# One PSUM bank or two for the two blocks of products of a weight tile, and four transposes ahead of their evictions

## The chip, the cores and the metric

The kernel runs on one core of a Trainium2 chip. The metric is the device time of one execution in microseconds (us); where several executions were timed, their median is given.

## The reference

Two blocks of two layers each, over one sequence of 256 tokens of width 1024. The first mixes a gated convolution with neighbourhood attention and ends each layer with a feed-forward part (dense in layer 0, eight experts with the best two taken in layer 1). The second has a window-and-context attention and a two-way matrix LSTM, and carries a context stream of another 256 tokens beside the latent one. Cut to what the change touches:

```
def first_block(x, p, ...):                       # layer i
    proj = h @ w_in[i] + b_in[i]                  # a, g (convolution), q, k, v
    conv_out = conformer_conv(a, g, ...)          # u = a * sigmoid(g), 31 taps
    attn_out = neighbourhood_attention(q, k, v, rpb[i])
    ...
def moe_swiglu(x, w_router, w1, w3, w2):          # layer 1: 8 experts
    y = (silu(xb @ w1[e]) * (xb @ w3[e])) @ w2[e]
    ...
def hybrid_layer(x, ctx, ..., last):
    xn = rmsnorm(x, norm_g) * (1 + scale_x) + shift_x
    cn = rmsnorm(ctx, norm_g) * (1 + scale_c) + shift_c
    aq, ak, av, az, mq, mk, mv, mo, mz, mi, mf = project(xn, w_in)
    caq, cak, cav, caz, cmq, cmk, ... = project(cn, w_in)
    q = rope_2d(aq); k = rope_2d(ak)
    att_x = window_ctx_attention(q, k, v, kc, vc, sink) * silu(az)
    xq, xk = silu(dwconv([mq, mk], conv_w, conv_b))     # 5 taps
    h_lat = mlstm_bidir(xq, xk, mv, mi, mf, ctx_state)
    ...
```

## The kernel before, in words

Every float32 product is made of three products of rounded parts: high by high, high by low and low by high (`mm3`). Weights come as raw tiles of 1 MB by DMAs that SyncE (SP) issues (L326). ScalarE (ACT) writes the high part, `whi` (L340), and VectorE (DVE) the low part, `wlo` (L341), in pieces of 1024 columns; two or three such split tiles exist at a time.

Where the result is wanted with channels on the partitions, a split tile of 1024 x 256 goes through `wstat`. It holds two blocks of 128 output channels, and each block is 8 x 3 = 24 products `gT` of 128x256, accumulated in PSUM. Then an eviction reads the block: ACT's sigmoid or DVE's `u` (L700) in the two mixers of the first block, ACT's `qraw` (L1633) for the queries and ACT's `up` (L1682) for the LSTM's q and k in the second. 45 weight tiles go this way, so there are 90 blocks: 16 tiles in the two mixers, 11 for the context (nine in its layer 0, two in its layer 1), 18 in the two latent layers of the second block.

The banks of `gT` come from the ring "a" of four PSUM banks (`bank`). Before the change, one bank is taken per weight tile and its halves hold the two blocks. Other products use the same ring: the token-major projections `gk`, the output projection `go`, the gates.

The order on each engine is fixed when the program is built: a scheduler places the instructions by priorities (`lift` raises those of evictions and of the chains behind them), and each engine runs its list in order. Where two engines touch one PSUM bank, the later one waits for the earlier on a semaphore. Behind the query blocks a rotation product (`prope`, of `qraw`) goes to GpSimd (POOL; `rt`, L1593) and to ACT (`Q`, L1601). Behind the LSTM blocks DVE runs the five taps. In the mixers DVE runs 31 taps (`y`, L765) as work that fills its gaps, and the taps left over go through `cvu`, a copy of `u` made by 16 DMAs (L783), to products `pcy`.

The context's layers run inside the expert layer of the first block: experts' weights (`sraw`, four buffers of 1 MB) stream in all the while, and their products `su` and `sy` fill TensorE's gaps. The context's norm, `norm_T`, is called once per context layer. It turns the normalized rows with transposes `ptT`, four to a bank over four banks, and ACT (`xhi`, L1502) and DVE (`xu`, L1503) read each half of a bank (256 columns, two transposes).

Of the kernel before, what the change touches and what calls it, by code (L numbers as in the profile page):

```python
# [23 lines left out]
P = 128  # L24
T = 256
# [145 lines left out]
class Kern:  # L171
# [201 lines left out]
            yield 1, lambda p0=p0: self.wload(w2d, 0, 8, c0 + p0, 256), lambda w, p0=p0: self.wstat(w, X, evict, p0 // P)  # L373

    def wstat(self, w, X, evict, b0):
        pt = self.bank("a", "gT")
        for bb in range(2):
            ps, cs = pt[:, bb * 256:(bb + 1) * 256], slice(bb * P, (bb + 1) * P)
            for k in range(8):
                self.mm3(ps, w[0][:, k, cs], w[1][:, k, cs], X.hi[:, k], X.lo[:, k], k == 0, k == 7)  # L380
            while self.pend:
                self.pend.popleft()[1]()
            with self.lift():
                evict(b0 + bb, ps)
# [1098 lines left out]
    def norm_T(self, l, s, x, xn, X, tag, keep=None):  # L1483


        nc, mods = self.nc, self.mods[l]
        if s:
            for t in range(2):
                self.rms(x[:, t], xn[t], self.hp.tile([P, D], F32, name="junk", tag="pT"))
        for j in range(4):  # L1490
            pt = self.bank(tag, "ptT")
            ks = slice(2 * j, 2 * j + 2)
            if keep is None:
                u = self.hp.tile([P, 512], F32, name="xu", tag="AT", bufs=2).rearrange("p (k t) -> p k t", k=2)
            else:
                u = keep[:, ks]
            for kk in range(2):
                k = 2 * j + kk
                a, b, ps = mods[:, s, 8 + k:9 + k], mods[:, s, k:k + 1], pt[:, kk * T:(kk + 1) * T]
                for t in range(2):  # L1500
                    self.turn_(ps[:, t * P:(t + 1) * P], xn[t][:, k * P:(k + 1) * P], self.ident)
                nc.scalar.activation(X.hi[:, k], ps, AF.Identity, scale=a, bias=b)  # L1502
                nc.vector.tensor_scalar(u[:, kk], ps, a, b, op0=ALU.mult, op1=ALU.add)  # L1503
            nc.vector.tensor_sub(X.lo[:, ks], u, X.hi[:, ks])
# [724 lines left out]
```

## Time and profile before

| | us |
|---|---|
| three runs | 2059.68, 2062.71, 2063.76 |
| their median | 2062.71 |
| the profiled execution, its own time | 2059.87 |
| its span, first to last instruction | 2058.1 |

The profiled execution is one more execution beside the three; all durations quoted from the trace are its own. Its span leaves 1.8 us outside. TensorE (PE) is busy for 93% of the span, DVE for 67%, ACT for 49%, POOL for 4%. The mean granted clock of TensorE is 0.972 of full speed.

### The profile page before, as it was taken

What the parts mean: (1) busy time and instruction counts of PE and PEld (TensorE: products, weight loads), DVE (VectorE), ACT (ScalarE), POOL (GpSimd) and SP (SyncE); (2) the same over time, 40 slices, a digit from 0 to 9 for tenths busy, and PEclk for the clock granted to TensorE, in tenths of its full rate; (3) what the DMA queues carried; (4) which work ended last, traced back from release to release, by engine and by line L of the source; (5) the groups of instructions that cost most, each with busy time, mean ns of one, the idle gap of its engine ahead of it and who ended that gap; (6) DMA issues with size and microseconds to landing.
All of it is one profiled execution on the core that took longest, in us unless ns stands there. A gap on an engine that the chain in (4) does not pass through costs nothing. (4 is left out here: it accounts for less than half of the span.)

```text
span 2058.1 us, 34210 instructions
## 1 busy us (share of the span) xinstructions
PE 1913.0 (93%) x13442; PEld 1526.5 (74%) x13442; DVE 1374.8 (67%) x2557; ACT 1012.2 (49%) x1663; POOL 81.8 (4%) x164
## 2 busy tenths in 40 slices
PE   6999999899887899788999999999999988998997
PEld 6768889687655565556877887887887868876886
DVE  8767444786646535564444444888888888887977
ACT  4534444335424323243333334777767745865774
POOL 1000000100100000000000000000000012011100
PEclk9999999899899999999999999999999999999999
DMA  8558776653689899999999996999999964334330
GB/s 291 171 187 295 265 263 207 204 188 123 231 343 324 305 357 305 342 370 350 370 381 394 377 340 244 342 353 328 353 332 336 326 202 141 103 109 123 103 103 32
DMA packets 276315, 541.06 MB, mean 263 GB/s; under 512 B 10912, under 2 KB 124336, under 8 KB 275888
## 3 DMA queue, kind: packets, MB, share of 16 engines
q1 hardware_dynamic: 274736, 534.73, 74.3%
q0 software_dynamic: 1120, 3.72, 0.6%
q8 instruction: 108, 1.77, 0.4%
q14 instruction: 63, 0.52, 0.1%
q10 hardware_dynamic: 288, 0.33, 0.0%
HBM read 533.26 MB, written 1.05 MB: 260 GB/s over the span
## 5 line engine op out<-in xcount | busy, mean ns | idle before, releaser
L341 DVE TENSOR_TENSOR wlo<-wraw,whi 128x1024 fp32r<-128x1024 f32 x572 | 681.9, 1230 | 184.7 <-ACT whi L340 181.2
L340 ACT ACTIVATE whi<-wraw 128x1024 fp32r<-128x1024 f32 x572 | 574.9, 1052 | 258.1 <-PE gT L353 47.5
L353 PE MATMUL gT<-xhi,whi 128*128 128x256 f32 x720 | 216.1, 302 | 19.7 <-ACT up L1682 8.6
L353 PE MATMUL gT<-xhi,wlo 128*128 128x256 f32 x720 | 209.9, 293 | 2.8 <-DVE wlo L341 2.7
L353 PE MATMUL gT<-xlo,whi 128*128 128x256 f32 x720 | 210.3, 293 | 1.7 <-DVE xlo L452 0.9
L353 PEld LDWEIGHTS gT<-xhi,whi 128*128 128x128 f32 x720 | 141.8, 197 | 33.6 <-ACT up L1682 10.2
L353 PEld LDWEIGHTS gT<-xhi,wlo 128*128 128x128 f32 x720 | 141.5, 197 | 8.7 <-issue 4.9
L353 PEld LDWEIGHTS gT<-xlo,whi 128*128 128x128 f32 x720 | 142.1, 197 | 5.4 <-issue 2.5
L353 PE MATMUL su<-sraw,xs 128*32 128x256 f32 (+1 forms) x2048 | 126.6, 371 | 15.2 <-DMA sraw<-in_moe_w 14.6
L353 PE MATMUL h<-whi,xeh 128*128 128x512 f32 x336 | 131.6, 392 | 1.0 <-DVE z L1183 1.0
L353 PE MATMUL h<-wlo,xeh 128*128 128x512 f32 x336 | 131.7, 392 | 0.0
L353 PE MATMUL h<-whi,xel 128*128 128x512 f32 x336 | 131.5, 391 | 0.0
L353 PE MATMUL hps<-xeh,whi 128*128 128x256 f32 x448 | 128.1, 286 | 0.0
L353 PE MATMUL hps<-xel,whi 128*128 128x256 f32 x448 | 126.7, 283 | 0.0
L353 PE MATMUL hps<-xeh,wlo 128*128 128x256 f32 x448 | 126.6, 283 | 0.0
L353 PEld LDWEIGHTS su<-sraw,xs 128*32 128x32 f32 x2048 | 59.1, 113 | 61.7 <-DMA sraw<-in_moe_w 19.2
L919 DVE TENSOR_TENSOR gg<-gg,hps 128x256 f32<-128x256 f32 x50 | 20.9, 419 | 122.1 <-ACT gg L918 122.1
L353 PE MATMUL gk<-whi,xhi 128*128 128x512 f32 x240 | 99.7, 418 | 2.1 <-ACT whi L340 1.5
L353 PE MATMUL gk<-wlo,xhi 128*128 128x512 f32 x240 | 98.7, 411 | 2.4 <-DVE wlo L341 2.2
L353 PE MATMUL hps<-xhi,whi 128*128 128x256 f32 x352 | 100.2, 285 | 0.0
L353 PE MATMUL hps<-xlo,whi 128*128 128x256 f32 x352 | 99.6, 283 | 0.0
L353 PE MATMUL hps<-xhi,wlo 128*128 128x256 f32 x352 | 99.5, 283 | 0.0
(470 smaller groups left out, 3968.6 us busy)
## 6 DMA issues: line engine op xcount, KB each, us to landing
sraw<-in_moe_w SPq DMA_DIRECT2D x168, 1024.0 KB, 8.8
wraw<-in_moe_w SPq DMA_DIRECT2D x168, 1024.0 KB, 6.8
wraw<-in_w_in SPq DMA_DIRECT2D x58, 1024.0 KB, 7.0
wraw<-in_ffn_w SPq DMA_DIRECT2D x33, 1024.0 KB, 5.2
wraw<-in_w_ada SPq DMA_DIRECT2D x24, 1024.0 KB, 5.3
wraw<-in_w_out SPq DMA_DIRECT2D x14, 1024.0 KB, 5.2
wraw<-in_w_in SPq DMA_DIRECT2D x24, 512.0 KB, 5.3
wraw<-in_ple_gate_w SPq DMA_DIRECT2D x8, 1024.0 KB, 7.1
```

The source lines that it names most:

```text
L340: nc.scalar.activation(hi[:, a:b], raw[:, a:b], AF.Copy)
L341: i = nc.vector.tensor_sub(lo[:, a:b], raw[:, a:b], hi[:, a:b])
L353: return self.behind(self.nc.tensor.matmul(out, lhsT, rhs, start=start, stop=stop, **kw))
L919: nc.vector.tensor_mul(g, g, pt[:, 256:])
```

## The change

It changes two helpers. In `wstat`, the line that takes a bank moves into the loop over the two blocks: each block has the first 256 columns of a bank of its own, and the ring of four turns twice as fast. In `norm_T`, all four transposes of a bank are written ahead of its two pairs of evictions, where two transposes and their evictions stood before the next two.

```
     def wstat(self, w, X, evict, b0):
-        pt = self.bank("a", "gT")
         for bb in range(2):
-            ps, cs = pt[:, bb * 256:(bb + 1) * 256], slice(bb * P, (bb + 1) * P)
+            ps, cs = self.bank("a", "gT")[:, :T], slice(bb * P, (bb + 1) * P)
             for k in range(8):
                 self.mm3(ps, w[0][:, k, cs], w[1][:, k, cs], X.hi[:, k], X.lo[:, k], k == 0, k == 7)
             while self.pend:
...
             for kk in range(2):
+                k, ps = 2 * j + kk, pt[:, kk * T:(kk + 1) * T]
+                for t in range(2):
+                    self.turn_(ps[:, t * P:(t + 1) * P], xn[t][:, k * P:(k + 1) * P], self.ident)
+            for kk in range(2):
                 k = 2 * j + kk
                 a, b, ps = mods[:, s, 8 + k:9 + k], mods[:, s, k:k + 1], pt[:, kk * T:(kk + 1) * T]
-                for t in range(2):
-                    self.turn_(ps[:, t * P:(t + 1) * P], xn[t][:, k * P:(k + 1) * P], self.ident)
                 nc.scalar.activation(X.hi[:, k], ps, AF.Identity, scale=a, bias=b)
                 nc.vector.tensor_scalar(u[:, kk], ps, a, b, op0=ALU.mult, op1=ALU.add)
```

Each engine has the same instructions in the same number before and after (14503 on PE, 2175 on ACT, 3217 on DVE, 173 on POOL and 1475 on SP, all kinds counted). Only their order and their waits differ. Lines from 377 to 1493 of the kernel have numbers lower by one after the change, lines past the middle of `norm_T` higher by one.

First place: PE in the second block's latent layer 0, at the first two blocks of the LSTM's q and k (one weight tile), with the rotation `prope` of the last query block between them. The names in brackets are the engines whose semaphores an instruction waits for. Before:

```order
L353 MATMUL gT<-xhi,whi 128x256
L353 MATMUL gT<-xlo,whi 128x256
L353 MATMUL gT<-xhi,wlo 128x256
L353 MATMUL prope<-qraw,const_20867 128x256 [waits DVE_49,Activation_49]
L356 MATMUL pcols<-const_88,rows 128x36 [waits DVE_49]
L356 MATMUL pcols<-const_88,rows 128x36 x2
L353 MATMUL gT<-xhi,whi 128x256 [waits Activation_49]
L353 MATMUL gT<-xlo,whi 128x256
```

The same place after the change:

```order
L353 MATMUL gT<-xhi,whi 128x256
L353 MATMUL gT<-xlo,whi 128x256
L353 MATMUL gT<-xhi,wlo 128x256
L353 MATMUL prope<-qraw,const_20894 128x256 [waits DVE_49,Activation_49]
L353 MATMUL gT<-xhi,whi 128x256
L353 MATMUL gT<-xlo,whi 128x256
L353 MATMUL gT<-xhi,wlo 128x256
L353 MATMUL gT<-xhi,whi 128x256
```

The second block, behind `prope`, no longer waits for ACT, and it stands ahead of the transposes `pcols` (the LSTM's gate rows), which now follow its 24 products.

Second place: ACT in the same stretch of the same layer; `rows` and `r_dl` belong to the gates. Before:

```order
L1633 ACTIVATE qraw<-gT 128x256
L340 ACTIVATE whi<-wraw 128x1024
L1633 ACTIVATE qraw<-gT 128x256
L1601 ACTIVATE Q<-rt 64x256 x2
L1956 ACT_TABLE_LOAD
L1956 ACTIVATE rows<-rows 36x256
L1957 ACTIVATE rows<-rows 36x256
L1959 ACTIVATE r_dl<-r_dl 36x2
L340 ACTIVATE whi<-wraw 128x1024 x2
L1633 ACTIVATE qraw<-gT 128x256
L1601 ACTIVATE Q<-rt 64x256 x4
L1682 ACTIVATE up<-gT 128x256
```

After:

```order
L1634 ACTIVATE qraw<-gT 128x256
L340 ACTIVATE whi<-wraw 128x1024
L1602 ACTIVATE Q<-rt 64x256 x2
L1634 ACTIVATE qraw<-gT 128x256
L1957 ACT_TABLE_LOAD
L1957 ACTIVATE rows<-rows 36x256
L1958 ACTIVATE rows<-rows 36x256
L1960 ACTIVATE r_dl<-r_dl 36x2
L340 ACTIVATE whi<-wraw 128x1024
L1634 ACTIVATE qraw<-gT 128x256
L1602 ACTIVATE Q<-rt 64x256 x4
L1959 ACTIVATE rows<-rows 36x256
```

The eviction `qraw` of the third query block has moved behind the pair `Q`, and a conversion `whi` and the eviction `up` have moved behind the last of the `rows`.

Third place: SP in the mixer of layer 0, where the copies `cvu` of the taps' input are issued; `in_w_in` is the mixer's weight. Before:

```order
L691 DMA z_66<-in_p 128x2x256
L326 DMA wraw<-in_w_in 128x4x512
L783 DMA cvu<-u 32x2x284 x16
L490 DMA row<-in_b_in 128x512
L326 DMA wraw<-in_w_in 128x4x512
```

After:

```order
L690 DMA z_66<-in_p 128x2x256
L782 DMA cvu<-u 32x2x284 x16
L326 DMA wraw<-in_w_in 128x4x512
L489 DMA row<-in_b_in 128x512
L326 DMA wraw<-in_w_in 128x4x512
```

The 16 copies have moved ahead of one weight tile in SP's queue.

## Rows read from the trace of the kernel before

**Rows 1.** Page, part 1: busy time, share of the span, and instructions per engine.
```profile
PE 1913.0 (93%) x13442; PEld 1526.5 (74%) x13442; DVE 1374.8 (67%) x2557; ACT 1012.2 (49%) x1663; POOL 81.8 (4%) x164
```

**Rows 2.** Waits of PE: who, for whom: us in total, times, longest.
```profile
PE su L353 <- DMA sraw<-in_moe_w: 14.6, 13, 1.9
PE gT L353 <- ACT up L1682: 8.6, 6, 3.7
PE gT L353 <- ACT qraw L1633: 4.8, 3, 2.5
PE gT L353 <- DVE u L700: 2.8, 2, 1.6
PE gT L353 <- DVE xlo L1504: 0.8, 1, 0.8
PE gT L353 <- ACT xhi L1502: 0.4, 1, 0.4
```

**Rows 3.** Windows, gT alone: us, PE, PEld, DVE, ACT busy, clock, DMA share, GB/s.
```profile
1728.90:1732.10 3.20, 3.09 (x23) 2.88 (x23) 0.00 (x0) 0.00 (x0) 1.00 1.02 286
1738.70:1743.75 5.05, 4.96 (x24) 4.76 (x24) 0.00 (x0) 0.01 (x1) 0.58 0.43 120
1913.40:1918.10 4.70, 4.63 (x24) 4.42 (x24) 0.00 (x0) 0.01 (x1) 0.64 0.33 94
923.90:928.50 4.60, 4.54 (x24) 4.34 (x24) 0.00 (x0) 0.00 (x0) 0.65 0.52 209
```

**Rows 4.** Windows, all work: the same columns, with POOL's busy time ahead of the clock.
```profile
33.00:63.00 30.00, 27.70 (x224) 26.89 (x224) 29.70 (x52) 13.05 (x18) 2.79 (x1) 1.00 0.57 173
400.00:520.00 120.00, 114.89 (x883) 95.40 (x882) 93.24 (x181) 53.51 (x103) 5.92 (x12) 0.98 0.53 170
585.00:760.00 175.00, 152.74 (x1420) 104.62 (x1420) 87.20 (x227) 60.55 (x141) 4.09 (x24) 0.94 0.91 324
920.00:940.00 20.00, 13.29 (x136) 8.66 (x135) 9.27 (x28) 5.16 (x13) 0.72 (x6) 0.85 0.79 311
1740.00:1780.00 40.00, 39.93 (x298) 35.24 (x299) 37.43 (x92) 31.41 (x69) 1.77 (x14) 0.96 0.33 106
1920.00:1960.00 40.00, 39.45 (x298) 34.11 (x297) 38.23 (x91) 33.02 (x72) 3.31 (x16) 1.00 0.31 103
```

**Rows 5.** Timeline, mixer of layer 0: start, us, engine, instruction [idle before, releaser].
```profile
51.08 10.38 SPq L783 DMA_DIRECT2D cvu<-u  x16
...
67.02 0.62 PE L353 MATMUL pcy<-cvu,cvw 128*32 128x256 f32 x2
...
81.95 0.39 PE L353 MATMUL gk<-whi,xhi 128*128 128x512 f32 x1
```

**Rows 6.** Page, part 6, DMA issues: count, KB each, median us to landing.
```profile
wraw<-in_w_in SPq DMA_DIRECT2D x58, 1024.0 KB, 7.0
...
cvu<-u SPq DMA_DIRECT2D x32, 71.0 KB, 2.1
```

**Rows 7.** Timeline, context layer 1, its last block of `gT`.
```profile
923.53 0.36 ACT L1682 ACTIVATE up<-gT 128x256 f32<-128x256 f32 x1
923.94 0.58 PE L353 MATMUL gT<-xhi,whi 128*128 128x256 f32 x1 [3.14 <-ACT up L1682]
...
933.25 0.66 PE L356 MATMUL pk<-const,kc 128*128 128x128 f32 x4 [0.36 <-DVE gcols L1967]
```

**Rows 8.** Timeline, latent layers 0 (first four rows) and 1 (last row).
```profile
1728.72 0.86 ACT L1601 ACTIVATE Q<-rt 64x256 fp32r<-64x256 f32 x2 [3.06 <-POOL rt L1593]
...
1737.45 0.85 ACT L1601 ACTIVATE Q<-rt 64x256 fp32r<-64x256 f32 x2 [1.15 <-POOL up L1681]
...
1738.33 0.38 ACT L1682 ACTIVATE up<-gT 128x256 f32<-128x256 f32 x1
...
1738.76 0.58 PE L353 MATMUL gT<-xhi,whi 128*128 128x256 f32 x1 [3.73 <-ACT up L1682]
...
1913.46 0.48 PE L353 MATMUL gT<-xhi,whi 128*128 128x256 f32 x1 [2.52 <-ACT qraw L1633]
```

More of the change, by code (lines that the diff above doesn't have):

```diff
@@ L375, in wstat @@
     def wstat(self, w, X, evict, b0):
-        pt = self.bank("a", "gT")
         for bb in range(2):
-            ps, cs = pt[:, bb * 256:(bb + 1) * 256], slice(bb * P, (bb + 1) * P)
+            ps, cs = self.bank("a", "gT")[:, :T], slice(bb * P, (bb + 1) * P)
             for k in range(8):
@@ L1497, in norm_T @@
             for kk in range(2):
+                k, ps = 2 * j + kk, pt[:, kk * T:(kk + 1) * T]
+                for t in range(2):
+                    self.turn_(ps[:, t * P:(t + 1) * P], xn[t][:, k * P:(k + 1) * P], self.ident)
+            for kk in range(2):
                 k = 2 * j + kk
                 a, b, ps = mods[:, s, 8 + k:9 + k], mods[:, s, k:k + 1], pt[:, kk * T:(kk + 1) * T]
-                for t in range(2):
-                    self.turn_(ps[:, t * P:(t + 1) * P], xn[t][:, k * P:(k + 1) * P], self.ident)
                 nc.scalar.activation(X.hi[:, k], ps, AF.Identity, scale=a, bias=b)
```

## The prediction

> **What bounds the kernel now.** I read the page's busy times first, then PE's waits, then windows of the stretches in which `gT` runs, then the timeline around the longest waits. PE is busy for 93% of the span [rows 1], so the kernel is TensorE-bound on the average and a shorter time has to come out of PE's idle 7% or out of products that run slowly. But the stages differ. In the mixer's window 33 to 63 DVE is busy for 29.70 of 30 us; in the context's windows the DMAs are at 0.91, and PE waits 14.6 us in all for `sraw`; in the latent layers DVE has 37.43 and 38.23 of 40 us while PE has nearly as much [rows 2, 4]. So a wait taken from PE is worth its length only where DVE or the DMAs do not set the pace anyway.
>
> PE's waits name what the one bank costs: products of `gT` wait 8.6 us for `up`, 4.8 for `qraw` and 2.8 for `u`, 16.2 us in 11 waits [rows 2]. The releasers are the evictions of the block before, and the timeline shows the shape: `up` ends at 1738.71, and the first product starts at 1738.76 after 3.73 us of idling [rows 8].
>
> Behind the long waits the products also run slowly. 24 products take 4.96, 4.63 and 4.54 us at a granted clock of 0.58 to 0.65, where 23 took 3.09 at 1.00 [rows 3]. For 24 that is 3.09 x 24 / 23 = 3.22, so the three long waits cost 1.74 + 1.41 + 1.32 = 4.5 us more. At clock 0.58 most of the block ran at the lower of the two levels (1.2 of 2.4 GHz), and what PE did before the fall was to idle 3.73 us.
>
> **The change part by part.** No instruction is added or removed, so nothing has a cost of its own; only waits and order count.
>
> *Own banks.* Before, a tile's second block waits for the eviction of the block just before it. After, a block waits for the one four blocks back. The latest eviction that I rest on is the `up` of 1738.33; it was held up by `Q` at 1737.45, which waits for POOL [rows 8]. Four banks give an eviction three blocks, 3 x 3.22 = 9.7 us, before anyone waits for it, so I take the new bank waits as 0. The faster ring could reach `gk` and `go`, which take two or four banks, but their last bank waited for the last block's eviction before as well: 0.
>
> *norm_T.* The transposes no longer wait for the evictions of the same bank. Products beside the two norms wait 0.8 us for `xlo` and 0.4 for `xhi` [rows 2]; I count 1.2 us in context layer 0 and nothing in layer 1.
>
> *What is on offer, and what I keep, by place.*
>
> Mixer of layer 0: 2.8 us offered (`u`). DVE is full for 30 us there [rows 4], and the products also need DVE's splits. There is a new wait as well: PE's order brings `pcy` some 20 products forward, 20 x 3.22 / 24 = 2.7 us, so with the waits gone it is due at 67.02 - 2.7 - 2.8 = 61.5, while the last copy `cvu` is issued at 61.46 and lands 2.1 us later [rows 5, 6]. That is a wait of up to 2.1, so 0.7 to 2.8 is left; I take 1.5. The weight tile now behind the copies in SP's queue is issued at about 61.5 and lands by 61.5 + 7.0 = 68.5; `gk` starts at 81.95 [rows 5, 6], so it has 13 us and costs nothing. If that cover were gone, the price would be its landing time, 7 us.
>
> Mixer of layer 1: no wait of this kind, 0 offered.
>
> Context layer 0: about 1.8 us of `up`'s 8.6 is left over for the other four waits (8.6 less 3.73 and 3.14, [rows 2, 7, 8]); I place half here, with the norm's 1.2: 2.1 offered. The DMAs are at 0.91 [rows 4]: bounds 0.2 (the other 9%) and 2.1; I take 1.5, because DMAs just below full leave a short wait recoverable.
>
> Context layer 1: 3.14 + 0.5 + 1.32 = 5.0 offered. The DMA share falls to 0.79 in 920 to 940, just where PE idles [rows 4], so about 0.21 x 20 = 4.2 us of DMA time is lost there and could be won. But the tail goes on to `pk` at 933.25, which waits for DVE [rows 7]. Bounds 0 and 5.0; I take half, 2.5.
>
> Latent layer 0: 3.73 + 0.2 + 1.74 = 5.7 offered. The second block now runs ahead of `pcols`, so what is late next is that gate chain, by up to one block (3.2 us), and the third query's `qraw`, which has moved behind a `Q` that waited 3.06 us for POOL [rows 8]. PE has 24 products to run meanwhile, so I put that new wait at 0 to 1.3 us. DVE idles only 2.6 us in 1740 to 1780 [rows 4], which is what can be drawn forward there. Bounds 0 and 5.7; I take 3, DVE's idle time and a little from the stretch ahead.
>
> Latent layer 1: 4.6 + 0.3 + 1.41 = 6.3 offered (of `qraw`, all but 0.2 is here; the last row shows 2.52). DVE idles 1.8 us in 1920 to 1960 [rows 4]. Bounds 0 and 6.3; I take 3, by the same reading.
>
> Sum kept: 1.5 + 1.5 + 2.5 + 3 + 3 = 11.5 us. Sum offered: 2.8 + 2.1 + 5.0 + 5.7 + 6.3 = 21.9 us. The profiled execution would go from 2059.9 to 2048.4. The median of the three runs lies 2.8 us higher, so against it the forecast is 2062.7 - 11.5 = 2051.2, say **2051 us**. The runs span 4.1 us, 0.2%, and that is about what a measurement of this kernel can tell from no change.
>
> **The rivals.**
>
> *All of it is kept.* PE is the bound everywhere and the other engines follow: 2062.7 - 21.9 = 2040.8. For it: PE's 93%. Against it: DVE's 29.70 of 30 and 38.23 of 40, and the full DMA queues [rows 4].
>
> *The wait moves.* DVE, POOL's rotation, `cvu` or the `sraw` stream takes over at each place, and PE idles as long one step later. In the context the order now has 48 `gT` in a row at three places where `su` products stood between the blocks. Those release the `sraw` buffers, so each place may stop the stream for one block: 3 x 3.2 = 9.6 us. With the context's gain gone too (4.0) that is 2062.7 - 7.5 + 9.6 = 2064.8; without it the wait moves for 2062.7. Against it: PE waits for `sraw` [rows 2], so the four buffers are mostly in flight rather than full. Time 2059 to 2066.
>
> *The change does not do what it says*, some other dependence holding the second block. The order shows the wait on ACT gone at the first place in the listing, so I give it nothing beyond the case before.
>
> *Slower, by order.* The scheduler pulls freed blocks ahead of the products on which the slow chains hang: `pcols` in latent layer 0 is an example. Each such block delays a chain by 3.2 us, and if PE then idles for the chain's end, the place loses instead of winning. At the six places where PE now waits longest, 6 x 3.2 = 19.2 against 11.5: 2062.7 + 7.7 = 2070. It decides from five places on (5 x 3.2 = 16 is more than 11.5 + 4.1). For it: ACT's and DVE's full queues in the latent layers. Against it: the queue at PE is not idle meanwhile, and each chain has a block of cover.
>
> *Slower, by the clock.* The blocks go round four banks instead of staying two to a bank, and TensorE's clock falls between them. A block at the low clock costs 1.74 us more [rows 3]. If that came to one block in four, 22 x 1.74 = 38: 2062.7 - 11.5 + 38 = 2089; from nine blocks (9 x 1.74 = 15.7) the change is slower. Against it: in every row with a low clock PE had idled for an eviction first, and in the mixer of layer 1, with no such wait, the clock is 0.98 for 120 us [rows 4].
> The Trainium skill, "TensorE: Matmul & The Clock Gate", section "A second HAM failure mode: psum-queue depth-cycling", is why this rival stands here: it tells of a kernel that cycled through PSUM banks and whose clock swung between its levels because PE idled briefly between groups. By that rule the time would go up; the trace so far agrees with its idling, which the old form has and the new one should lose, and no row shows cycling alone to do it.
>
> **How the numbers follow.** Forecast, part kept: 0.48, with a range of its own of 2046 to 2057 (16 to 6 us of the 21.9). All kept: 0.14. The wait moves: 0.22. Slower by order: 0.10; by the clock: 0.06. Faster by over 0.2% (below 2058.6) is the first two, 0.62; within 0.2%, 0.22; slower, 0.16. The first three cases hold 0.84, and they reach from 2038 (all kept, with the 2.8 us by which executions differ) to 2066, which is the range.
>
> **What would show it.** Right: PE's waits of `gT` for `up`, `qraw` and `u` fall from 16.2 us to under 3; the blocks behind 1738, 1913 and 923 take about 3.2 us at clock 1.00; the latent layers end some 3 us earlier each, and the DMA share at 920 to 940 rises. Wrong on the mixer: `pcy` waits for `cvu` by more than 2 us. Wrong on the latents: `prope`, `pcols` or `sc` wait for ACT, DVE or POOL as long as `gT` did. Wrong on the context: the expert stage is as long as before, with PE waiting longer for `sraw`. The prediction as a whole is wrong if the freed time comes back as DVE or DMA waits in every stage, or if blocks of `gT` run at the low clock with no wait ahead of them.

## The result and the profile after

The changed kernel takes 2051.7 us (median of 6 runs, 2046.4 to 2053.8), the kernel before 2062.2 (6 runs, 2059.7 to 2063.8). The ratio is 0.9943, 95% interval 0.9929 to 0.9956: 11.8 us faster (9.1 to 14.6), where 11.5 was forecast; the two medians lie 10.5 us apart. The profiled execution took 2053.8 us, the slowest of the six, with a span of 2052.0.

The page's first part, which answers to [rows 1]:

```profile
PE 1912.5 (93%) x13442; PEld 1532.2 (75%) x13442; DVE 1373.8 (67%) x2557; ACT 1012.0 (49%) x1663; POOL 81.7 (4%) x164
```

PE's waits after the change (product, releaser: us in total, times, longest). The groups of [rows 2] for `up`, `qraw`, `u` and the context's `xlo` and `xhi` are gone; these are what `gT` still waits for, and the chief waits of other products that are new or longer:

```profile
PE su L353 <- DMA sraw<-in_moe_w: 15.6, 12, 2.5
...
PE prope L353 <- ACT qraw L1634: 4.4, 3, 2.4
PE gT L353 <- DVEq L1090: 4.1, 1, 4.1
...
PE pdec L353 <- DVE dg L1971: 3.6, 1, 3.6
...
PE gT L353 <- DVE wlo L341: 3.3, 3, 1.3
...
PE pk L356 <- DVE gcols L1968: 2.6, 1, 2.6
...
PE sc L353 <- DVE gcols L1968: 1.6, 1, 1.6
PE gT L353 <- ACT whi L340: 1.5, 2, 1.3
...
PE sc L353 <- DVE rt L1592: 1.4, 1, 1.4
...
PE pcols L356 <- ACT rows L1959: 1.2, 1, 1.2
```

So some 17 us of waits went, and some 12 came up elsewhere: `prope`, `pdec`, `pk`, `sc` (for `gcols` and `rt`) and `pcols` have 14.8 us, and had 2.6 before. The windows say where that matters (us, then PE, PEld, DVE, ACT, POOL busy, granted clock, DMA share, GB/s). The first two answer to rows of [rows 4]; as the changed kernel is some 7 us ahead at the start of the context's layer 1 and 10 at its end, the third shows about the work that stood at 920 to 940 before:

```profile
33.00:63.00 30.00, 29.70 (x240) 27.54 (x239) 29.96 (x55) 11.49 (x17) 2.88 (x1) 1.00 0.55 165
920.00:940.00 20.00, 13.54 (x127) 6.22 (x120) 6.00 (x16) 2.40 (x6) 0.46 (x2) 0.77 1.01 373
910.50:930.50 20.00, 15.52 (x172) 10.08 (x171) 11.66 (x35) 6.11 (x15) 0.72 (x6) 0.91 0.99 376
1700.00:1745.00 45.00, 37.68 (x273) 34.66 (x273) 39.20 (x95) 27.59 (x55) 12.83 (x21) 0.92 0.37 109
```

In the mixer PE went from 27.70 to 29.70 of 30 us, with DVE as full as before. For the work of 920 to 940 before, the DMA share rose from 0.79 to 0.99 and PE's busy time from 13.29 to 15.52 us. In the stretch 1700 to 1745 of latent layer 0 PE still idles 7.3 us of 45.

Since each run below left a trace too, a stage's length can be read in 14 executions, as the time between the first starts of two products in the timeline (the first transposes and the first `hps` bound mixer 0; the last `hps` of layer 0 and the first `plg` mixer 1; the 48th of the 96 `go` of the context's layer 0 and the 1201st `hps` the context's layer 1 with its tail; the first latent `pgate` and the transposes at 1870 latent layer 0; the rest is latent layer 1). Worked out from the timelines, means in us:

```
stage               one bank per tile   a bank per block   difference
mixer 0             165.6 (5 traces)    160.0 (8)          -5.6
mixer 1             156.3 (5)           155.2 (8)          -1.1
context layer 1     116.9 (4)           113.1 (8)          -3.8
latent layer 0      179.9 (8)           180.8 (3)          +0.9
latent layer 1      188.2 (8)           190.5 (3)          +2.3
```

(The context's rows have the new norm beside the new banks. Kernels of the last experiments are in a row only where they leave its stage as the whole change or as before.) Within a row and column the traces of the latent layers agree to 1 us, those of the mixers to 3.4, those of the context to 4. The context's layer 0, from the first `su` to the same `go`, isn't listed: with the change it took 293 to 297 us in four traces and 305 to 306 in four, against 299 to 300 before, and one kernel showed both. It goes with TensorE's clock, whose mean over the stage is 0.931 to 0.942 in the four short ones and 0.894 to 0.900 in the four long ones. Among the traces at 0.931 or 0.932 the old form took 298.9, 299.0 and 299.3 us and the new one 296.7, 295.9 and 296.1: 2.9 us less.

### The profile page after: what moved, and what is told of

Its sections match the earlier page's. It is cut to its first block, busy times and chain, and to the rows that moved or that the text cites. A ratio compares the mean times of both kernels' runs of the same rounds, so it can differ in the third digit from the quotient of the medians.

```text
span 2052.0 us, 34198 instructions
## 1 busy us (share of the span) xinstructions
PE 1912.5 (93%) x13442; PEld 1532.2 (75%) x13442; DVE 1373.8 (67%) x2557; ACT 1012.0 (49%) x1663; POOL 81.7 (4%) x164
## 5 line engine op out<-in xcount | busy, mean ns | idle before, releaser
L353 PE MATMUL gT<-xhi,whi 128*128 128x256 f32 x720 | 211.6, 296 | 1.5 <-ACT whi L340 1.5
L353 PE MATMUL su<-sraw,xs 128*32 128x256 f32 (+1 forms) x2048 | 126.4, 374 | 16.1 <-DMA sraw<-in_moe_w 15.6
```

Source lines behind the costliest of these rows:

```text
L353: return self.behind(self.nc.tensor.matmul(out, lhsT, rhs, start=start, stop=stop, **kw))
```

## The experiments

All ratios are to the kernel before, on the same chip and in the same session.

**Parts by place.** `wstat` gets a word for its caller, and only the named callers take a bank per block. The order on PE is that of before with no caller named, and that of the change with all:

```
-    def wstat(self, w, X, evict, b0):
+    def wstat(self, w, X, evict, b0, part):
+        own = part in ("mix",)            # e2: ("ctx",)  e3: ("lat",)  e4, e6: ("ctx", "mix")
         for bb in range(2):
-            ps, cs = self.bank("a", "gT")[:, :T], slice(bb * P, (bb + 1) * P)
+            if own or bb == 0:
+                pt = self.bank("a", "gT")
+            lo = 0 if own else bb * 256
+            ps, cs = pt[:, lo:lo + 256], slice(bb * P, (bb + 1) * P)
```

The first, the mixers alone (A is the theory that the time comes where the traces part, B the forecast's own terms, C scatter):

> Two banks per weight tile in the two mixers alone; the context, the latent layers and the context's norm as before. Theory A (the time of the change comes where the two traces part: -5.2 us by the end of the first mixer, -2.1 in the second): 7.3 us faster than before, some 2055. Theory B (the sum of the prediction: 1.5 us in the mixers): 2060.7, not to be told from before. Theory C (what the two traces show by place is the scatter of single executions, above all of the moment at which TensorE's clock rises): between -3 and +1.

Measured: 0.9962 (0.9947 to 0.9977), 7.9 us faster. A holds; the forecast's 1.5 for the mixers and C are out.

> Two banks per weight tile for the context's blocks, and the context's norm with its four transposes first; mixers and latent layers as before. Theory A (the two traces part by 3.0 us at the context's layer 1, by nothing at layer 0): 3 us faster, some 2059. Theory B (1.5 + 2.5): 4 us faster, 2058. Theory C: within 2 us of before. A and B agree here; C is what this run tells them from.

Measured: 0.9966 (0.9952 to 0.9979), 7.0 us faster (4.3 to 9.9). C is out; A and B were both low.

> Two banks per weight tile in the two latent layers alone; the rest as before. Theory A (the latent layers lose 1.2 and 2.4 us between the two traces: DVE's chain and the rotation set their length, and the waits only move to prope, pcols and pdec): 0 to 3.6 us slower than before, 2062 to 2066. Theory B (3 + 3): 6 us faster, 2056. Theory C: within 2 us of before. In its trace, by A, PE waits for qraw and dg as long in the latent layers as it waited for up and qraw before, some 7 us in all; by B less than 2 us.

Measured: 1.0000 (0.9991 to 1.0010): no gain. B's 6 us is out; the time can't tell A from C. Its trace has the latent layers 1.0 and 2.4 us longer than the mean with one bank, and PE waits there for `prope`, `pcols` and `pdec` by 2.45, 1.25 and 3.63 us, as after the change, 7.3 us in layer 0, about what A had.

> The change everywhere but in the two latent layers. Theory A: the 7.3 us of the mixers and the 3 us of the context together, 10.3 faster, some 2052, and as fast as the whole change or up to 3.6 us faster. Theory B: 5.5 us faster, 2056.7, so 6 us slower than the whole change. Theory C: the parts do not add up.

Measured: 0.9913 (0.9899 to 0.9928), 18 us faster (15 to 21). More than A's sum; the next pair was to say whether the latent layers cost that much.

> The changed kernel once more, beside the next three on one chip. By its earlier ratio of 0.9943: 11.7 us faster than before. Theory A says that its latent layers take back what the mixers and the context win: it is then 4 to 8 us slower than the next run. Theory D (the latent layers are a draw, as they were alone, and 0.9913 without them was a lucky chip): the same as the next run within 3 us.

Measured: 0.9935 (0.9912 to 0.9958).

> The change everywhere but in the latent layers, a second time. Theory A: ratio near 0.9913 again, 16 to 18 us faster than before and 4 to 8 faster than the whole change. Theory D: near 0.994, as the whole change.

Measured: 0.9925 (0.9906 to 0.9944). On one chip the two are 2 us apart, within both intervals: D holds for the times. The traces still show 3 us lost in the latent layers, which the intervals of these two runs can't tell from nothing. This version is not shown to beat the change.

**Banks or norm, in the context.** e7 takes banks for the context and keeps the old norm; e8 is the second half of the diff alone.

> Two banks for the context's blocks alone, with the norm as before. The context with its norm was 7 us faster. If the banks do it (waits of 0.9 us in layer 0, 3.1 and 0.5 with 1.3 of slow clock in layer 1): 5 to 7 faster. If the norm does it: 0 to 2 faster.

> The context's norm with its four transposes first, and nothing else of the change. By the forecast's terms 1.2 us faster in layer 0 and nothing in layer 1, so not to be told from before; if the norm is what the context gains by, 5 to 7 faster.

Measured: banks 0.9978 (0.9962 to 0.9993), 4.5 us faster; norm 0.9991 (0.9976 to 1.0007), not told from before. The banks give the larger part of e2's 7.0; whether the norm gives the rest stays open, since its own interval reaches from 5.0 us faster to 1.4 slower.

**The wait put back.** Two banks in the mixers as in e1, and a semaphore in place of the shared bank:

```
+                if own and bb and k == 0:
+                    i = self.mm(ps, a_[0], b_[0], True, False)
+                    self.tc.add_manual_dep(i.ins, ev.ins.name, SYNC, reason="the first block's eviction goes first")
...
-                evict(b0 + bb, ps)
+                ev = evict(b0 + bb, ps)
```

> Two banks per tile in the mixers, as in the first run, but the first product of a second block waits on a semaphore for the eviction of the first block, as it did when both lay in one bank. If the removed wait is what the mixers gain by: the 8 us are lost again, so 2 us either side of before; and more, up to 8 us slower than before, because the blocks are now run strictly one after the other where the scheduler had filled some of the wait with the next tile's first products. If the gain comes from anything else (the banks as such, the places of the evictions on ACT and DVE): still some 8 us faster than before.

Measured: 1.0051 (1.0032 to 1.0070), 10.5 us slower than before and 18 slower than e1, from which it differs by the semaphore and the order that follows from it. So a second bank gains nothing while the wait stands. That is 2.5 us beyond the most that was expected: PE now waits ahead of six second blocks in each mixer, and the second mixer, which had no listed wait of `gT` before, took 164.1 us instead of 156.3. PE's waits in its first mixer, 18 to 130:

```profile
PE gT L354 <- DVE u L711: 4.3, 2, 3.1
...
PE gT L354 <- ACT sig L709: 1.2, 2, 0.6
...
PE gT L354 <- ACT z L726: 1.1, 2, 0.6
```

In the kernel before, only the two waits for `u` are listed there: the scheduler had put one to ten products of the next tile ahead of each of these blocks. So this run is not the old order with its old wait. It shows that the wait costs time and the bank alone brings none; it doesn't measure that the wait's removal is the whole 7.9 us.

**What holds the latent layers.** Three kernels, each the whole change and one edit:

```
# e10, in rope:
+            with self.lift():
                 V.tensor_mul(t2, pr[:, :T], self.C("sin"))
                 G.tensor_mul(dst, src, self.C("cos"))
                 G.tensor_add(dst, dst, t2)
# e11, in stack_q (e12 leaves the line out, and zeroes Q on POOL when it is allocated):
-                V.tensor_sub(H.Q[oth, g, v], q[own], H.Q[own, g, v])
+                G.tensor_sub(H.Q[oth, g, v], q[own], H.Q[own, g, v])
```

> The whole change, and the rotation's three operations (on DVE and POOL) get the evictions' priority, so that on DVE they stand ahead of the LSTM's gate scans. In the latent layers of the changed kernel PE waits 2.4 us for qraw, which stands on ACT behind Q, which waits for the rotation, which waits on DVE behind scans; then 1.2 for rows and 3.6 for dg, the end of the gate chain. If the rotation is what holds PE: those 2.4 us and the 1.8 of the other layer go, 3 to 4 us faster than the whole change. If DVE's sum of work holds it: the wait for dg grows by what the wait for qraw loses, and the time is that of the whole change within 2 us.

Measured: 0.9934 (0.9918 to 0.9950), the time of the whole change. In layer 0 the wait for `dg` fell from 3.6 to 0.2 us and that for `qraw` rose from 2.4 to 5.5, so the edit moved the wait the other way round; the layer took 179.1 us, 1.7 less than the mean with a bank per block, and layer 1 190.3. Neither expectation came: the rotation's place on DVE alone doesn't set the time.

> The whole change, with the eight subtractions per latent layer that write the low half of Q moved from DVE (0.42 to 0.53 us each, 4.2 in the stretch 1700 to 1740) to POOL. If DVE's sum of work sets the pace in the latent layers while PE waits: each layer ends 2 to 4 us earlier, 4 to 8 in all against the whole change. If the rotation's chain through POOL and ACT sets it: POOL, which runs the rotation too, gets later, and the kernel is 0 to 5 us slower than the whole change.

Measured: 0.9942 (0.9924 to 0.9960). Layer 0 took 182.5 us, layer 1 189.5, together 0.7 us more than with the whole change. The 4 to 8 us faster are out; the second expectation, 0 to 5 us slower, can't be told from a draw.

> The whole change, with the eight subtractions per latent layer for the low half of Q left out (the low half is zero, written by POOL ahead of the queries): 4.2 us of DVE work less per layer, and nothing put in its place in the rotation's chain. From the start of the latent layers' gate products to the end of the layer the traces give 180.6 to 180.9 us for layer 0 of the whole change, and 180.3 to 180.6 for layer 1. If DVE's sum of work sets the pace where PE waits: 3 to 4 us less in each. If the chain of rotation and gates through ACT, POOL and DVE does, with DVE's work beside it: less than 1 us less.

Measured: 0.9942 (0.9926 to 0.9957). The time is that of the whole change. In the one trace layer 1 took 185.7 us where the whole change has 190.5, as DVE's sum of work would have it; layer 0 did not gain (182.3). There the wait for `qraw` is untouched, and the rest has moved to `sc` (PE's waits, 1700 to 1760):

```profile
PE sc L353 <- DVE rt L1592: 2.6, 1, 2.6
PE prope L353 <- ACT qraw L1633: 2.4, 1, 2.4
PE sc L353 <- DVE gcols L1969: 1.2, 1, 1.2
PE pcols L356 <- ACT rows L1960: 0.2, 1, 0.2
```

## Why the prediction was right, and where its terms were not

The sum was right within 1 us (11.5 against 11.8 by the ratio and 10.5 between the medians), and so was that no bank wait would take the old one's place: no wait of `gT` for an eviction is listed any more. But that the sum was so near is luck: it holds two errors that cancel. Of the forecast's five terms, the three for the mixer and the context were too small and the two for the latent layers had no gain behind them.

**The mixers: 1.5 + 0 forecast, 7.9 measured (4.8 to 10.9), 6.7 in the traces.** The step that failed is "DVE is full for 30 us there, and the products also need DVE's splits", from which I kept half. DVE is still full after (29.96 of 30) and PE now has 29.70 busy [rows 4 for before]. About half of what filled DVE (15.3 us of 29.70) were taps `y`, for which no product of the next block waits. DVE's taps in that window, before and after (instructions, then us busy and mean ns):

```profile
L765 DVE SCALAR_TENSOR_TENSOR y<-u,cols,y 128x256 f32<-128x256 f32 x36 | 15.3, 478 | 0.1
L764 DVE SCALAR_TENSOR_TENSOR y<-u,cols,y 128x256 f32<-128x256 f32 x42 | 19.6, 532 | 0.0
```

The splits `wlo`, which PE needs, came no later: the eight that ended between 33.5 and 53.8 before ended 1.9 to 4.4 us earlier after. So DVE's full time bounded nothing here; only the part of it that somebody waits for could have.

The offer itself was undersized as well. Beside the listed 2.8 us there are stalls too short for the list. In the timeline of before a second block starts 0.29 us after the product ahead of it, where the spacing is 0.12, and no wait is printed:

```profile
39.09 0.28 PE L353 MATMUL gT<-xlo,whi 128*128 128x256 f32 x1
39.21 0.28 PE L353 MATMUL gT<-xhi,wlo 128*128 128x256 f32 x1
39.50 0.39 PE L353 MATMUL gT<-xhi,whi 128*128 128x256 f32 x1
```

Three such places (0.30, 0.27 and 0.37 us), and the product behind each, which comes 0.22 us later instead of 0.12, add 0.9 us in mixer 0. In the trace of after there are none at these blocks. Over the stage, PE idles 9.4 to 9.9 us in the five traces with one bank and 6.4 to 6.8 in the eight with two: the waits are 3 us of the 5.6, and products that follow closer or at a higher clock the rest. Mixer 1, for which I offered nothing because no wait of it is listed, has three such places too (0.31, 0.25 and 0.37 us). But it took 153.8 to 156.8 us with own banks, at granted clocks of 0.948 to 0.924, so what its 1.1 us are made of isn't shown. And in three of the five traces with one bank in the mixers, the wait for `u` is one of 3.1 us with a fall of the clock behind it, which the trace I had did not show. In the trace of e2, the wait, and the window of the products around it:

```profile
46.64 0.39 PE L353 MATMUL gT<-xhi,whi 128*128 128x256 f32 x1 [3.12 <-DVE u L703]
```

```profile
46.00:52.00 6.00, 5.36 (x32) 5.37 (x33) 0.96 (x2) 0.00 (x0) 0.72 0.07 25
```

The mean granted clock of 0.72 over that window means that over half of it was at the lower of the two levels. The new wait of up to 2.1 us that I had put against the gain, `pcy` for `cvu`, didn't come: PE idles 0.30 us ahead of the first `pcy`, and the trace names no releaser for it. The weight tile behind the copies cost nothing, as said.

**The context: 4.0 forecast, 7.0 measured (4.3 to 9.9).** The mechanism was right and the sizes too small. The DMA queue fills the hole at 920 to 940, and layer 1 with its tail is 3.8 us shorter where 2.5 was the term. `pk` waits 2.6 us for DVE after (0.36 before, [rows 7]), the part that I had taken off. Layer 0 is 2.9 us shorter among the six traces at one clock, where 1.5 was the term and 2.1 the offer; what made it more than the offer isn't shown. The rival that 48 `gT` in a row stop the `sraw` stream is not borne out: `su` and `sy` wait 15.6 + 5.1 = 20.7 us for it, and waited 14.6 + 6.6 = 21.2 before.

**The latent layers: 3 + 3 forecast, nothing measured (2 us either way), 3.2 us longer in the traces.** Here the rival that the wait moves is what happened, and its sign was there: over the two layers `gT` had waited 8.9 us, and `prope`, `pcols`, `pdec` and `sc` now wait 12.2, of which 2.2 stood there before. The step that failed is "DVE's idle time and a little from the stretch ahead" as what can be drawn forward.

In layer 0 PE waited 3.7 + 2.0 + 0.2 = 5.9 us in the stretch and now waits 2.45 + 1.25 + 3.63 = 7.3. The timeline after the change shows one link (POOL, DVE, ACT and PE; in brackets the idle time ahead and its releaser):

```profile
1718.69 0.76 POOL L1594 TENSOR_TENSOR rt<-rt,rt 128x256 f32<-128x256 f32 x1 [6.40 <-DVE rt L1592]
...
1719.49 0.85 ACT L1602 ACTIVATE Q<-rt 64x256 fp32r<-64x256 f32 x2 [3.81 <-POOL rt L1594]
...
1720.36 0.38 ACT L1634 ACTIVATE qraw<-gT 128x256 f32<-128x256 f32 x1
...
1720.80 0.48 PE L353 MATMUL prope<-qraw,const 128*128 128x256 f32 x1 [2.45 <-ACT qraw L1634]
...
1733.53 0.64 PE L353 MATMUL pdec<-dg,ones 36*128 36x36 f32 x2 [3.63 <-DVE dg L1971]
```

The rotation's `rt` ended on DVE at 1718.5, behind the gates' scans and a split. `Q` on ACT waits for it, the next `qraw` stands behind `Q`, and PE is out of products it may run: it has finished in the meantime the blocks on which it used to wait. I had seen `qraw` move behind `Q` and priced it at 0 to 1.3 us, because "PE has 24 products to run meanwhile". PE had run them, and the third query's wait is 2.45; the fourth query's, 2.0 before, went in exchange. The larger part is the gate chain, which I had named as late "by up to one block (3.2 us)": 1.25 + 3.63 = 4.9. Its end, `dg`, which `pdec` needs, is where it was. On DVE before, with the layer's first gate product `pgate` at 1690.55, and after, with `pgate` at 1681.16:

```profile
1741.71 0.70 DVE L1970 TENSOR_SCALAR dg<-const,r_dl 36x36 f32<-36x36 f32 x1
1732.78 0.70 DVE L1971 TENSOR_SCALAR dg<-const,r_dl 36x36 f32<-36x36 f32 x1
```

`dg` ends 51.8 to 51.9 us behind `pgate` in all eight traces with one bank and 52.3 to 52.4 in the three with two. PE used to spend the time up to it on the second block at the low clock; now that block is done, and PE idles. In e11 and e12, with the subtractions off DVE, `dg` ends at 45.1 and 44.3, so what DVE runs in front of it sets its end. But then PE waits for the rotation (`qraw` 2.5 and 2.4, `rt` 2.6 in each), and in e10, which hurries the rotation, for `qraw` again. So in layer 0 two chains, the gates' and the rotation's, run through DVE, POOL and ACT, and freeing one brings up the other. That rests on one trace of each edit.

Layer 1 is longer for another reason: PE idles no longer there, but its products run slower. The whole layer, before and after (us, PE, PEld, DVE, ACT, POOL busy, clock, DMA share, GB/s), and below, `gT` alone, the block of after at the place of the one at 1913.40 in [rows 3]:

```profile
1870.20:2058.10 187.90, 168.13 (x1074) 143.02 (x1074) 148.49 (x377) 118.17 (x255) 14.45 (x28) 0.97 0.29 88
1861.70:2052.00 190.30, 171.33 (x1074) 145.08 (x1074) 148.14 (x377) 117.62 (x255) 13.34 (x28) 0.93 0.30 86
```

```profile
1905.90:1910.45 4.55, 4.51 (x24) 4.50 (x24) 0.00 (x0) 0.38 (x1) 0.62 0.39 103
```

PE idles 19.0 us instead of 19.8 and is busy 3.2 us longer, at a granted clock of 0.93 instead of 0.97; all three traces with two banks have 0.932 or 0.933, the eight with one 0.947 to 0.970. The clock falls behind the new waits, 1.8 us of `prope` and then 1.4 and 1.6 of `sc`, and it is low for 10.2 us at the layer's start where it was low for 3.4 (two of the eight traces with one bank have 10.2 there too). The block above still takes 4.51 us, so the 1.41 us that I had counted for its clock did not come back. In e12, layer 1 has 3 us less idling (16.1) and a clock of 0.951: that is how it gets 4.8 us shorter by leaving out 4.2 us of DVE's work.

**The clock.** Two of the three slow blocks of [rows 3] now run at full clock: in latent layer 0 the 24 products at 1724.60 take 3.16 us at 1.00, and in the context the 48 from 909.5 to 915.5 run at 1.00 without a stop. The third, in latent layer 1, doesn't. The mean granted clock of the two profiled executions is 0.972 and 0.965, but that is scatter: it is 0.964 to 0.972 over 64 executions of the kernel before and 0.961 to 0.972 over 12 of the changed one, 0.967 on the mean of either. The rival that cycling through banks lowers it is not borne out: in the mixers of the changed kernel the clock, once risen, is low for `gT` only at the start of the second one (for 6 products, and 12 before), and e6, with own banks for 27 of 45 tiles, has 0.972 too. In latent layer 1, where two banks go with a lower clock, an idle stretch stands ahead of each fall. The Trainium skill, "TensorE: Matmul & The Clock Gate", section "A second HAM failure mode: psum-queue depth-cycling", puts such swings down to short idling between groups; here the trace agrees with the idling, and the mixers show no cost of cycling without it.

## What to carry to other kernels

Two accumulations that share a PSUM bank run one after the other with an eviction between them. In the mixers here a second bank was worth more than the waits that the profile lists, since products that start 0.3 to 0.4 us apart at a boundary, where 0.12 is the spacing, and the clock behind long waits came on top; in the latent layers it was worth nothing, since PE reached the end of another chain earlier and waited there. Before a wait's price is cut because another engine is full, look at what fills that engine: filler that nobody waits for moves out of the way, a serial chain does not. Look at PE's idle time and at its clock apart, because a stage can get longer with no more idling. And a sum that comes out right says nothing about its terms; runs by place do.

## What the runs showed of the hardware

One kernel's executions differ by 10 us and more (2047.2 to 2064.7 for e4), and TensorE's clock is a large part of it. The same kernel's traces on two chips, e6 and e4, over the context's layer 0, from the first `su` to the 48th `go`:

```profile
555.90:852.00 296.10, 253.79 (x2265) 169.06 (x2265) 149.31 (x380) 94.83 (x214) 6.57 (x29) 0.93 0.92 328
```

```profile
561.50:867.90 306.40, 262.84 (x2265) 176.18 (x2265) 149.48 (x380) 94.58 (x215) 6.59 (x29) 0.89 0.90 317
```

With the clock at 0.89 instead of 0.93, the same 2265 products kept PE busy 9.1 us longer, and PE idled 43.6 us instead of 42.3. That is 10.3 of the 17.6 us by which the two executions' spans differ. The first rise of the clock scatters too, with the same work ahead of it: products of mixer 0 are spaced 0.21 us apart until 26.0 in the trace of before and until 22.6 in that of after (28 and 40 products in the same 6 us), and over the 14 traces the clock first rose between 20.1 and 26.4 us. So a difference of 2 or 3 us between two single traces may be the clock's alone, and a stage is to be read from several.
